# Strassen branch a: storing only the sums of blocks, and splitting the plain blocks during attention

## The chip, the cores and the metric

The kernel runs on one core of one Trainium2 chip. The metric is the device time of one execution in microseconds (us), the median of a few runs.

## The reference

One layer of a hybrid block: an RMS norm, a mixer with two branches, a residual, another RMS norm, a SwiGLU feed-forward layer and a second residual. S = D = 1024, eight heads of 64, all in float32. Cut to the mixer, which is what the change touches:

```python
def mixer(h, w_in, b_f, conv_w, w_branch, w_out):
    proj = jnp.einsum("bsd,dn->bsn", h, w_in)
    q, k, v, f_logit, g_b, g_c, hc, gate_conv, gate_attn = jnp.split(proj, _SPLITS, axis=-1)
    ya = g_b * causal_depthwise_conv(g_c * hc, conv_w)             # 1024 x 512
    yb = forgetting_attention(q, k, v, log_sigmoid(f_logit + b_f)) # 1024 x 512
    ya_d = jnp.einsum("bsc,cd->bsd", ya, w_branch[0])              # branch a
    yb_d = jnp.einsum("bsc,cd->bsd", yb, w_branch[1])              # branch b
    merged = jax.nn.sigmoid(gate_conv) * ya_d + jax.nn.sigmoid(gate_attn) * yb_d
    return jnp.einsum("bsd,de->bse", merged, w_out)
```

## The kernel before

**Numbers.** A float32 product is made of three passes: each operand is kept as a high half and a low half, and `mm3` (line 126) multiplies high by high, high by low and low by high. The halves come from `split` (line 121): ScalarE copies the source to the high half, VectorE subtracts the high half from the source. Most large products, branch a's among them, are also done by Strassen's scheme: seven products of half-size blocks in place of eight, three of them with a plain block on the weight side (A11, A12, A22) and four with sums of blocks (S1 to S4); likewise on the data side, B11, B21, B22 and T1 to T4.

**Stages.** (1) Norm of the input and the projection to v. (2) The other projections: 18 jobs (numbered 0 to 17; 0 to 3 give q and k, 4 to 9 the convolution branch, 10 to 17 the gates), each one call of `strassen` (line 681) of 84 matmuls of 512 columns. The weights of a job are loaded raw from `w_in` in two transfers, `raw_t` (three buffers), while the job before it runs; VectorE forms their sums (tile `sx`) and both engines split them. (3) Attention, in 21 steps t = 0 to 20 with two more for the rest; steps 0 and 1 run inside job 17. In each step from 2 on there are score matmuls (`sp`), transposes (`tps`), the product with v (`po`) and one chunk of branch a's product (`pba`, six matmuls by `a_chunk`, line 1401); six more chunks, `A_TAIL`, come behind the last step. (4) Branch b's product (`pbb`), the merge, w_out, and the feed-forward layer. Stage 4 is not touched.

**Work beside the projections.** TensorE runs job after job in stage 2. Beside it VectorE, ScalarE and the queues prepare operands that later stages need, in small steps. The table at line 1213 says behind which addition of which job a step stands: (j, 0) is behind the first `c12` addition of job j, some 5 us into it, and (j, 1) behind the last `c21` addition at its end. `wa_steps` (762) makes branch a's weight operands from `w_branch`, `ya_steps` (819) its data operands from `ya_dram`, both in two halves k, and `wo_steps` (715) the operands of w_out in four parts. Each loads rows, forms sums, splits, and stores both halves from the GpSimd queue (`wa_dram`, `ya_ops`, `wt_dram`, `w22_dram`). The tiles are few: `r0`, `l0` and `h0` (one buffer each), `yh` and the four rows of `rows4`. So a load of the next part waits until the store of the part before has landed, and since the loads stand on SyncE's queue (SP), what is queued behind them there, the weights of the next job among it, waits with them.

**Order in attention.** From the last job to the end of attention, the instructions of every engine stand in the order in which they are written (`strict[0] = engines`, lines 1285 and 1352); elsewhere only marked VectorE work does, and a scheduler orders the rest. Three tables say what a step does besides: `chunks` (1510, which product), `cuts` (1558, which splits) and `at` (loads and others). Before the change `load_y` and `load_w` fetch all seven operands of either side ready, halves included: 1 MB for one of data, 256 KB for a quarter of one of weights.

Of the kernel before, what the change touches and what calls it, by code (L numbers as in the profile page):

```python
# [46 lines left out]
def block_kernel(  # L47
# [706 lines left out]

    def load_rows(src):
        for n, rows_ in enumerate(src):
            nc.sync.dma_start(rows4[:, n], rows_)

    def wa_rows(k):
        return [w_branch[0, 0][r * P : (r + 1) * P, :] for r in (k, k + 2)]  # L760

    def wa_steps(k):

        def of(op, n):
            return lambda t: wa_dram[op : op + n, :, t, k, :].rearrange("o p c -> p o c")

        tags = deque(("r0", "l0", "h0") * 2)

        def out(op, t):
            n = t.shape[1]  # L770
            h = half_tile(w0_tile(tags.popleft()))[:, :n]
            copy(h, t)
            strict[0] = ("vector",)
            sub(t.bitcast(F32R), t, f32(h))
            strict[0] = ()
            nc.gpsimd.dma_start(of(op, n)(0), f32(h))
            nc.gpsimd.dma_start(of(op, n)(1), t)
# [12 lines left out]
        yield  # L790
        h, l = (half_tile(w0_tile(tags.popleft())) for _ in range(2))
        h4, l4 = (t.rearrange("p o (q c) -> p o q c", q=4) for t in (h, l))
        for n, t in enumerate((a, b)):
            copy(h4[:, n], t[:, 0])
            strict[0] = ("vector",)
            sub(l4[:, n], t[:, 0], f32(h4[:, n]))
            strict[0] = ()
        nc.gpsimd.dma_start(of(4, 2)(0), f32(h))
        nc.gpsimd.dma_start(of(4, 2)(1), f32(l))
        h = half_tile(w0_tile(tags.popleft()))  # L800
        h4 = h.rearrange("p o (q c) -> p o q c", q=4)
        copy(h4[:, 0], b[:, 1])
        strict[0] = ("vector",)
        sub(h4[:, 1], b[:, 1], f32(h4[:, 0]))
        strict[0] = ()
        for t in range(2):
            nc.gpsimd.dma_start(of(6, 1)(t), f32(h[:, t : t + 1]))
        yield
        out(0, s)
        yield  # L810
        if k == 0:
            load_rows(wa_rows(1))
        out(2, u)
        yield

# [3 lines left out]
    def ya_steps(k):  # L819

        def out(op, t):
            n = t.shape[1]
            h = half_tile(z_tile("yh", F32R).rearrange("p (a b) -> p a b", a=2))[:, :n]
            copy(h, t)
            strict[0] = ("vector",)
            sub(t.bitcast(F32R), t, f32(h))
            strict[0] = ()
            for w, x in ((0, f32(h)), (1, t)):
                nc.gpsimd.dma_start(
                    ya_ops[op : op + n, :, w, k, :].rearrange("o p c -> p o c"), x  # L830
                )
# [18 lines left out]
        yield  # L850
        out(2, u)
        yield
# [360 lines left out]
    for first, make in (  # L1213
        (((2, 0), (2, 1), (3, 0), (3, 1)), lambda: wa_steps(0)),
        (((4, 0), (4, 1), (5, 0), (5, 1)), lambda: wa_steps(1)),
        (((10, 1), (11, 0), (11, 1), (12, 0), (12, 1)), lambda: ya_steps(0)),
        (((13, 0), (13, 1), (14, 0), (14, 1), (15, 0)), lambda: ya_steps(1)),
        *(
            (((j, 0), (j, 1), (j + 1, 0), (j + 1, 1)), lambda k=k: wo_steps(k))
            for k, j in enumerate((7, 10, 12, 14))  # L1220
        ),
    ):
        it = make()
        for j, n in first:
            plans[j][n].append(it)
# [3 lines left out]
    for ij, (kind, j, _, _) in enumerate(jobs):  # L1229
# [40 lines left out]
        elif ij < len(jobs) - 1:  # L1270
            if ij == 10:
                load_rows(ya_rows(0))
# [87 lines left out]
    HOME = dict(B11="h0", B21="h1", T2="l0", T3="l1", T4="h0", T1="h1", B22="l1")  # L1360
    wring = deque()

    def load_y(o, queue=nc.sync):
        yops[o] = yq.tile([P, 2, 2, NC], F32R, tag=f"y{HOME[o]}", name=f"y{o}", bufs=1)
        queue.dma_start(f32(yops[o]), ya_ops[SUMS_Y.index(o)])

    def load_w(o, p):
        if not wring:
            wring.extend(("s4", "s4h", "s4h", "s4l", "s4l"))
        tag = wring.popleft()  # L1370
        wops[o, p] = wtile(tag, 1 if tag == "s4" else 2, F32R, (P, 4, P))
        nc.sync.dma_start(
            f32(wops[o, p]),
            wa_dram[SUMS_W.index(o)][:, :, :, p * P : (p + 1) * P].rearrange(
                "p t k c -> p (t k) c"
            ),
        )
# [147 lines left out]
    def next_w():  # L1525
# [3 lines left out]
        (0, 0), (2, 0), (4, 0), (6, 0), (1, 0), (3, 0), (5, 0), (1, 1), (0, 1),  # L1529
        (3, 1), (2, 1), (5, 1), (4, 1), (7, 1), (6, 1), (7, 0),  # L1530
    ])

    def next_sg():
# [25 lines left out]
    for j, parts in (  # L1559
# [18 lines left out]
    for t in (6, 8, 10, 13, 14, 20, 21, 22):  # L1578
        at[t].append(next_sg)
    at[15] += [do(cb_of, 3, 0, True), do(cb_of, 3, 1, True)]  # L1580
    for k, t in enumerate((13, 13, 16, 16)):
        at[t].append(do(load_wb, k))
    rows = {8: (0, None), 13: (1, None), 17: (2, None), 19: (3, 0)}
    for t, (j, part) in rows.items():
        at[t - 1].append(do(inverse, j, part))
        for n in range(2) if part is None else ():
            at[t + 2 + n * (j < 2)].append(do(divide, j, n))
    at[NU].append(do(divide, 3, 0))
# [4 lines left out]
    q_load(1)  # L1593
    load_y("B21")
    for _ in range(3):
        next_w()
# [3 lines left out]
    for t in range(2, NU + 2):  # L1600
# [6 lines left out]
        if t == NU:  # L1607
            early = [a_chunk(*c) for c in chunks.pop(t)]
        if 5 < t <= NU:
# [17 lines left out]
        if t == NU:  # L1627
            for m in early:
                m()
            inverse(3, 1)  # L1630
# [6 lines left out]
        if t > NU:  # L1637
            drain = inverse_rows(3, pss, "T", 2, 1)
            while lows:
                lows.pop(0)()  # L1640
            drain()
        if back:
            dc = turn_bank(back, 1, 0, "ACT" if wide else "DVE")
            dd = turn_bank(back, 1, 1, "DVE" if wide else "ACT")
        for i, e in now[1]:
            row_max(t, i, e)
        if back:
            dc()
# [32 lines left out]
    psm, psm_close = pool("psm2", 6, space=PSUM)  # L1681
    t1_close()

# [4 lines left out]

    TAIL_DONE = len(A_TAIL)
    yb2 = [halves_of(0)]  # L1690
    done = []
    for n, (what, p) in enumerate(A_TAIL):
# [5 lines left out]
        if n == 2:  # L1698
            for m in done[:2]:
                m()  # L1700
            for x in range(2):
                next_sg()
            done[2]()
        if n > 2:
            done[n]()
            if SGS:
                next_sg()
    for n in (1, 0):
# [16 lines left out]
    yb_split(1, range(4))  # L1725
    strict[0] = ()
    yb_close()
    wo_pool, wo_close = pool("wo", side="right")
# [783 lines left out]
```

## Time and profile before

| | |
|---|---|
| median of 3 runs | 1345.71 us (1344.67 to 1351.09) |
| the profiled execution | 1345.25 us, its span 1343.5 us |
| TensorE matmul (PE) | 1308.2 us, 97% of the span, 6671 instructions |
| TensorE weight load (PEld) | 1086.1 us, 81% |
| VectorE (DVE) | 947.5 us, 71% |
| ScalarE (ACT) | 564.5 us, 42% |
| GpSimd (POOL) | 210.4 us, 16% |
| DMA | 245.08 MB in packets, 182 GB/s in the mean |
| mean granted TensorE clock | 0.991 of full speed |

Times count from the start of the span, and 1.75 us of the execution lie outside of it. PE's busy time is not work at its peak: matmuls are pipelined, and back to back one of 512 columns shows 0.39 us but starts every 0.225 us. SP is the queue of SyncE, which here only starts transfers; a row with SPq is its sequencer. What ended an engine's idle time stands in square brackets. All instructions of the kernel bear line 76, the line of a helper, so that they are told apart by the names of their tiles: `b` are the accumulators of a projection job, `hB11`, `hT12` and so on its data operands, `c` its results, `pba` the accumulators of branch a, `um` its results.

### The profile page before, as it was taken

Reading aid. Unit: us, or ns where it says so; the run is one execution under the profiler, and the core shown is the slowest. Engines: PE = TensorE matmul, PEld = TensorE weight load, DVE = VectorE, ACT = ScalarE, POOL = GpSimd, SP = SyncE. Lnnn points to the kernel's source line nnn. Section 1 sums busy time; section 2 is a strip of 40 time slices with the busy share of each in tenths; the row PEclk is TensorE's granted clock in tenths of the full one; section 3 lists DMA queues with packets and bytes.
Section 4 is the critical chain, followed back from the end, with each engine's and each line's share of the span. In section 5 each row is a group of like instructions: output and inputs, shape, how many; then the busy total and the mean of one; then the engine's idle time right before and its main releaser. Section 6 shows DMA issues by size and latency. Waiting matters only on the chain.

```text
span 1343.5 us, 17834 instructions
## 1 busy us (share of the span) xinstructions
PE 1308.2 (97%) x6671; PEld 1086.1 (81%) x6671; DVE 947.5 (71%) x1352; ACT 564.5 (42%) x875; POOL 210.4 (16%) x382
## 2 busy tenths in 40 slices
PE   9999999997889999899999999999999999999998
PEld 8988788886668888778888888888888888888886
DVE  7876878785565677777767788876667656676575
ACT  7533323343334667422577532323222323444452
POOL 3112101122222222000223112210011011000001
PEclk9999999998989999999999999999999999999999
DMA  6355454466864864596467556542333236966541
GB/s 229 102 173 191 170 150 164 156 213 240 268 219 172 283 233 161 158 323 226 107 189 251 188 166 197 184 149 72 110 103 117 96 109 238 359 242 194 165 165 63
DMA packets 184198, 245.08 MB, mean 182 GB/s; under 512 B 12440, under 2 KB 125152, under 8 KB 183216
## 3 DMA queue, kind: packets, MB, share of 16 engines
q1 hardware_dynamic: 157904, 155.03, 36.9%
q0 software_dynamic: 26192, 88.92, 18.0%
q8 instruction: 52, 0.85, 0.3%
q14 instruction: 34, 0.28, 0.1%
q10 hardware_dynamic: 16, 0.00, 0.0%
HBM read 168.09 MB, written 75.83 MB: 182 GB/s over the span
## 4 chain that ended last, share of the span: by engine, by line
PE 72%; issue 18%; POOL 4%; DVE 2%; DMA 2%; ACT 1%; POOLq 0%; DVEq 0%; ACTq 0%; SPq 0%
PE b L76 40%; PE pd L76 16%; PE pbb L76 3%; PE pba L76 3%; PE tps L76 2%; PE po L76 2%; PE sp L76 2%; PE pv L76 1%; PE ma L76 1%; POOL sg_dram L76 1%; PE tp L76 1%; POOL ya_ops L76 1%; DVE lo L76 1%; DMA wa_dram<-r 1%; PE mb L76 1%
## 5 line engine op out<-in xcount | busy, mean ns | idle before, releaser
L76 DVE TENSOR_TENSOR c<-c,b 128x512 f32<-128x512 f32 x215 | 146.8, 683 | 74.2 <-PE b L76 71.4
L76 DVE TENSOR_TENSOR lo<-raw,hi 128x1024 fp32r<-128x1024 f32 (+1 forms) x91 | 109.6, 1205 | 70.5 <-PE b L76 53.1
L76 ACT ACTIVATE hi<-raw 128x1024 fp32r<-128x1024 f32 (+1 forms) x98 | 99.5, 1015 | 93.9 <-PE b L76 54.9
L76 ACT ACTIVATE hi<-sx 128x1024 fp32r<-128x1024 f32 x44 | 46.7, 1061 | 181.5 <-PE b L76 157.6
L76 DVE TENSOR_TENSOR sx<-raw 128x512 f32<-128x512 f32 x78 | 53.7, 689 | 51.8 <-issue 22.5
L76 DVE TENSOR_TENSOR lo<-sx,hi 128x1024 fp32r<-128x1024 f32 x44 | 53.8, 1223 | 38.8 <-PE b L76 31.2
L76 PE MATMUL b<-w12h,lo 128*128 128x512 f32 x208 | 80.9, 389 | 0.0
L76 PE MATMUL b<-w12h,hi 128*128 128x512 f32 x204 | 79.4, 389 | 0.0
L76 PE MATMUL b<-w12l,hi 128*128 128x512 f32 x204 | 79.4, 389 | 0.0
L76 PE MATMUL b<-hh,hi 128*128 128x512 f32 x176 | 69.0, 392 | 0.0
L76 PE MATMUL b<-hh,lo 128*128 128x512 f32 x176 | 68.5, 389 | 0.0
L76 PE MATMUL b<-hl,hi 128*128 128x512 f32 x176 | 68.5, 389 | 0.0
L76 PE MATMUL b<-hT12h,lo 128*128 128x512 f32 x136 | 55.0, 404 | 12.5 <-DVE lo L76 12.5
L76 PE MATMUL b<-w,s4h 128*128 128x512 f32 x208 | 64.1, 389 | 0.0
L76 PE MATMUL pd<-hi,lo 128*128 128x512 f32 x160 | 62.3, 389 | 0.0
L76 PE MATMUL pd<-hi 128*128 128x512 f32 x160 | 61.9, 390 | 0.0
L76 POOL DMA_DIRECT2D a_dramA<-um x33 | 17.9, 542 | 276.0 <-DVE um L76 275.4
L76 PE MATMUL b<-hT34h,hi 128*128 128x512 f32 x136 | 53.9, 396 | 7.3 <-DVE c L76 7.3
L76 PE MATMUL pd<-ghi 128*128 128x512 f32 x148 | 57.6, 390 | 0.0
L76 PE MATMUL pd<-glo,ghi 128*128 128x512 f32 x148 | 57.6, 389 | 0.0
L76 PE MATMUL pd<-ghi,glo 128*128 128x512 f32 x148 | 57.6, 389 | 0.0
L76 PE MATMUL b<-hT12l,hi 128*128 128x512 f32 x136 | 54.1, 398 | 0.0
(479 smaller groups left out, 3606.2 us busy)
## 6 DMA issues: line engine op xcount, KB each, us to landing
raw<-in_w_gate_up_dram SPq DMA_DIRECT2D x52, 512.0 KB, 3.9
raw<-in_w_in_dram SPq DMA_DIRECT2D x35, 512.0 KB, 4.3
a_dramS<-um POOLq DMA_DIRECT2D x44, 256.0 KB, 3.0
a_dramA<-um POOLq DMA_DIRECT2D x33, 256.0 KB, 2.6
sg<-sg_dram SPq DMA_DIRECT2D x32, 256.0 KB, 5.1
graw<-a_dramS SPq DMA_DIRECT2D x14, 512.0 KB, 3.8
sg_dram<-c POOLq DMA_DIRECT2D x24, 256.0 KB, 2.8
raw<-in_w_down_dram SPq DMA_DIRECT2D x11, 512.0 KB, 4.5
```

The source lines that it names most:

```text
L76: ins = getattr(self.engine, name)(*args, **kw)
```

## The change

Only the sums are now formed beside the projections and stored: S1 to S4 and T1 to T4. The plain blocks A11, A12, A22 and B11, B21, B22 are loaded raw in attention, from `w_branch` (tile `wraw`, five buffers of 128x256) and from `ya_dram` (tile `raw`, the ring of three that w_in's weights and the probabilities use), and halved there, a copy on ScalarE and a subtraction on VectorE: A blocks in the step before the one that multiplies with them, B21 in step 2, B22 in step 21, and B11 and the first quarter of A11 ahead of step 2. With fewer steps to place, the table of line 1213 is spaced anew: `wo_steps` starts in jobs 4, 7, 10 and 12 in place of 7, 10, 12 and 14 and takes two to four jobs a part, and `ya_steps` has four steps a half in place of five. The two loads of `ya_dram` rows for `ya_steps` move from SP's queue to GpSimd's. In the last steps of attention, four loads of gates move from the tail to step 17, the drains of the accumulators come ahead of other work of their step, and the divisions by the softmax sums come a step earlier for two of the heads' pairs.

```diff
-    wa_dram = dpool.tile([7, P, 2, 2, NC], F32, name="wa_dram")
-    ya_ops = dpool.tile([7, P, 2, 2, NC], F32, name="ya_ops")
+    wa_dram = dpool.tile([4, P, 2, 2, NC], F32, name="wa_dram")
+    ya_ops = dpool.tile([4, P, 2, 2, NC], F32, name="ya_ops")
...
-    SUMS_W = ("S3", "S2", "S1", "S4", "A11", "A12", "A22")
-    SUMS_Y = ("T1", "T3", "T2", "T4", "B21", "B22", "B11")
+    SUMS_W = ("S3", "S2", "S1", "S4")
+    SUMS_Y = ("T1", "T3", "T2", "T4")
...
+    def spill(dst, op, k, t, h):
+
+        copy(h, t)
+        strict[0] = ("vector",)
+        sub(t.bitcast(F32R), t, f32(h))
+        strict[0] = ()
+        for w, x in ((0, f32(h)), (1, t)):
+            nc.gpsimd.dma_start(dst[op : op + 2, :, w, k, :].rearrange("o p c -> p o c"), x)
...
         if k == 0:
             load_rows(wa_rows(1))
-        out(2, u)
+        spill(wa_dram, 0, k, s, half_tile(w0_tile(("r0", "h0")[k])))
+        yield
+        spill(wa_dram, 2, k, u, half_tile(w0_tile("l0")))
         yield
...
-        out(4, b)
-        out(6, a[:, :1])
+        spill(ya_ops, 0, k, t, staged())
         yield
         if k == 0:
-            load_rows(ya_rows(1))
-        out(0, t)
-        yield
-        out(2, u)
+            load_rows(ya_rows(1), nc.gpsimd)
+        spill(ya_ops, 2, k, u, staged())
...
-            (((j, 0), (j, 1), (j + 1, 0), (j + 1, 1)), lambda k=k: wo_steps(k))
-            for k, j in enumerate((7, 10, 12, 14))
+        (((12, 1), (13, 0), (13, 1), (14, 0)), lambda: wo_steps(3)),
...
+        raws[o] = half_tile(raw_t())
+        m, ns = dict(B11=(0, n1), B21=(2, n1), B22=(2, n2))[o]
+        for k in range(2):
+            queue.dma_start(raws[o][:, k], ya_dram[m + k][:, ns])
+
+    def split_y(o):
+        return halve(yops[o][:, 0], yops[o][:, 1], raws.pop(o))
+
+    def split_w(o, p):
+        w = wops[o, p]
+        return halve(w[:, :2], w[:, 2:], raws.pop((o, p)))
...
+    cuts[2].append(do(split_y, "B21"))
+    cuts[21].append(do(split_y, "B22"))
+    for t, list_ in list(chunks.items()):
+        for c in list_:
+            o = SEQ[c[0]][0]
+            if t > 2 and o not in SUMS_W:
+                cuts[t - 1].append(do(split_w, o, c[1]))
...
+    at[17].append(late_sgs)
...
     load_y("B21")
+    lows = [split_y("B11"), split_w("A11", 0)]
+    for low in lows:
+        low()
...
         if t > NU:
             drain = inverse_rows(3, pss, "T", 2, 1)
-            while lows:
-                lows.pop(0)()
+            for m in muls:
+                m()
+            at[t].pop(0)()
             drain()
+            muls = []
```

How this moves the instructions, at three places. First SP's queue in jobs 10 to 15: `r` and `l` are the rows of w_out, `rows` those of `ya_dram` (`ya_dram_73`, `ya_dram_71`) or of `c_dram`, and `raw<-in_w_in_dram` the weights of the next job. Before:

```order
L76 DMA raw<-in_w_in_dram 128x8x128 x3
L76 DMA r_2781<-in_w_out_dram 128x1024
L76 DMA raw<-in_w_in_dram 128x8x128
L76 DMA rows_970<-ya_dram_73 128x1024
L76 DMA rows_970<-ya_dram_71 128x1024
L76 DMA l_2783<-in_w_out_dram 128x1024
L76 DMA raw<-in_w_in_dram 128x8x128 x3
L76 DMA r_3085<-in_w_out_dram 128x1024
```

and now:

```order
L76 DMA raw<-in_w_in_dram 128x8x128 x4
L76 DMA r_2831<-in_w_out_dram 128x1024
L76 DMA l_2833<-in_w_out_dram 128x1024
L76 DMA raw<-in_w_in_dram 128x8x128 x4
L76 DMA rows_970<-c_dram 128x1024 x2
L76 DMA raw<-in_w_in_dram 128x8x128 x2
```

The two loads of `ya_dram` rows are gone from this queue, and of the loads of w_out's rows only one pair stands between the weights here, where there were two.

Second the same queue at the start of attention, from v's first load on; `yB` and `s` are operands of branch a, `cb` the bias rows, `lo` and the last `raw` k and q of the second pair of heads. Before:

```order
L76 DMA v_3505<-v_dram 128x8x128
L76 DMA yB_3672<-ya_ops 128x2048
L76 DMA s_3674<-wa_dram 128x4x128
L76 DMA cb<-c_dram 128x1024 x2
L76 DMA lo<-qk_dram_67 128x1024
L76 DMA v<-v_dram 128x8x128
L76 DMA raw<-qk_dram_67 128x1024
L76 DMA yB_3686<-ya_ops 128x2048
```

and now:

```order
L76 DMA v_3459<-v_dram 128x8x128
L76 DMA raw<-ya_dram_70 128x512
L76 DMA raw<-ya_dram_71 128x512
L76 DMA wraw<-in_w_branch_dram 128x2x128
L76 DMA cb<-c_dram 128x1024 x2
L76 DMA lo<-qk_dram_67 128x1024
L76 DMA v<-v_dram 128x8x128
L76 DMA raw<-qk_dram_67 128x1024
L76 DMA raw<-ya_dram_72 128x512
L76 DMA raw<-ya_dram_73 128x512
```

B11 and B21 now each take a buffer of the ring `raw`, and stand at the same place in the queue as the ready operands did.

Third VectorE in step 2 of attention, from the last copy of step 1's transposes on (`ISA` rows are the row maxima of the scores, which end in `nm`). Before:

```order
L76 COPY raw<-tps 128x512
L76 ISA rows_970,nm<-sp,rows_970 128x768
L76 ISA nm 128x1
L76 ISA rows_970,nm<-sp,yb 128x128
L76 ISA nm 128x1
L76 COPY ptT<-tps 128x384
```

and now:

```order
L76 COPY raw<-tps 128x512
L76 TENSOR_TENSOR yB_3626<-raw,yB_3626 128x1024
L76 TENSOR_TENSOR s_3630<-wraw,s_3630 128x256
L76 ISA rows_970,nm<-sp,rows_970 128x768
L76 ISA nm 128x1
L76 ISA rows_970,nm<-sp,yb 128x128
L76 ISA nm 128x1
```

The subtractions for B11 and A11 stand ahead of the row maxima of step 2 (on ScalarE their copies stand ahead of that step's first copy of transposes).

More of the change, by code (lines that the diff above doesn't have):

```diff
@@ L753, in quarter, with load_rows @@
         return rows4[:, n].rearrange("p (a b) -> p a b", a=2)
-    def load_rows(src):
+    def load_rows(src, queue=nc.sync):
         for n, rows_ in enumerate(src):
-            nc.sync.dma_start(rows4[:, n], rows_)
+            queue.dma_start(rows4[:, n], rows_)
     def wa_rows(k):
         return [w_branch[0, 0][r * P : (r + 1) * P, :] for r in (k, k + 2)]
-    def wa_steps(k):
[L764 to L777, printed above, removed]
+    def spill(dst, op, k, t, h):
[5 more added lines that the diff above has]
+            nc.gpsimd.dma_start(dst[op : op + 2, :, w, k, :].rearrange("o p c -> p o c"), x)
+    def wa_steps(k):
         a, b = (
@@ L790, in wa_steps @@
         yield
[L791 to L807, printed above, removed]
-        yield
-        out(0, s)
-        yield
         if k == 0:
             load_rows(wa_rows(1))
-        out(2, u)
+        spill(wa_dram, 0, k, s, half_tile(w0_tile(("r0", "h0")[k])))
+        yield
+        spill(wa_dram, 2, k, u, half_tile(w0_tile("l0")))
         yield
@@ L819, in ya_steps, with staged @@
     def ya_steps(k):
[L821 to L831, printed above, removed]
+        def staged():
+            return z_tile("yh", F32R).rearrange("p (a b) -> p a b", a=2)
         a, b, t, u = (quarter(n) for n in range(4))
@@ L1213, in block_kernel @@
     for first, make in (
[L1214 to L1218, printed above, removed]
-            (((j, 0), (j, 1), (j + 1, 0), (j + 1, 1)), lambda k=k: wo_steps(k))
-            for k, j in enumerate((7, 10, 12, 14))
-        ),
+        (((2, 0), (2, 1), (3, 0)), lambda: wa_steps(0)),
+        (((3, 1), (4, 0), (4, 1)), lambda: wa_steps(1)),
+        (((4, 1), (5, 0), (5, 1), (7, 0)), lambda: wo_steps(0)),
+        (((7, 1), (8, 0), (8, 1), (10, 0)), lambda: wo_steps(1)),
+        (((10, 1), (11, 0), (11, 1), (12, 0)), lambda: wo_steps(2)),
+        (((12, 1), (13, 0), (13, 1), (14, 0)), lambda: wo_steps(3)),
+        (((10, 1), (11, 1), (12, 0), (12, 1)), lambda: ya_steps(0)),
+        (((13, 1), (14, 0), (14, 1), (15, 0)), lambda: ya_steps(1)),
     ):
@@ L1271, in block_kernel @@
             if ij == 10:
-                load_rows(ya_rows(0))
+                load_rows(ya_rows(0), nc.gpsimd)
             if ij == 16:
@@ L1360, in block_kernel @@
     HOME = dict(B11="h0", B21="h1", T2="l0", T3="l1", T4="h0", T1="h1", B22="l1")
-    wring = deque()
+    wring, raws = deque(), {}
     def load_y(o, queue=nc.sync):
-        yops[o] = yq.tile([P, 2, 2, NC], F32R, tag=f"y{HOME[o]}", name=f"y{o}", bufs=1)
-        queue.dma_start(f32(yops[o]), ya_ops[SUMS_Y.index(o)])
+        yops[o] = t = yq.tile(
+            [P, 2, 2, NC], F32R, tag=f"y{HOME[o]}", name=f"y{o}", bufs=1
+        )
+        if o in SUMS_Y:
+            queue.dma_start(f32(t), ya_ops[SUMS_Y.index(o)])
+            return
+        raws[o] = half_tile(raw_t())
[7 more added lines that the diff above has]
+        return halve(w[:, :2], w[:, 2:], raws.pop((o, p)))
     def load_w(o, p):
@@ L1371, in load_w @@
         wops[o, p] = wtile(tag, 1 if tag == "s4" else 2, F32R, (P, 4, P))
+        if o in SUMS_W:
+            nc.sync.dma_start(
+                f32(wops[o, p]),
+                wa_dram[SUMS_W.index(o)][:, :, :, p * P : (p + 1) * P].rearrange(
+                    "p t k c -> p (t k) c"
+                ),
+            )
+            return
+        m, c = (0 if o == "A11" else 2), (2 * p + (o == "A22")) * P
+        raws[o, p] = t1.tile([P, 2, P], F32, tag="wraw", name="wraw", bufs=5)
         nc.sync.dma_start(
[L1373 to L1376, printed above, removed]
+            raws[o, p],
+            w_branch[0, 0][m * P : (m + 2) * P, c : c + P].rearrange("(k p) c -> p k c", p=P),
         )
@@ L1529, in block_kernel, with late_sgs @@
         (0, 0), (2, 0), (4, 0), (6, 0), (1, 0), (3, 0), (5, 0), (1, 1), (0, 1),
-        (3, 1), (2, 1), (5, 1), (4, 1), (7, 1), (6, 1), (7, 0),
+        (3, 1), (5, 1), (2, 1),
     ])
+    def late_sgs():
+        for ds_ in ((7, 7), (4, 6)):
+            t = t1.tile([P, S], F32, tag="cb", name="sg", bufs=2)
+            for d, n in zip(ds_, range(2)):
+                sgs[d, n if d == 7 else 1] = t[:, (n1, n2)[n]]
+                nc.sync.dma_start(
+                    sgs[d, n if d == 7 else 1], sg_dram[d][0][:, (n1, n2)[n if d == 7 else 1]]
+                )
     def next_sg():
@@ L1607, in block_kernel @@
         if t == NU:
-            early = [a_chunk(*c) for c in chunks.pop(t)]
+            for m in [a_chunk(*c) for c in chunks.pop(t)]:
+                m()
         if 5 < t <= NU:
@@ L1627, in block_kernel @@
         if t == NU:
-            for m in early:
-                m()
             inverse(3, 1)
@@ L1646, in block_kernel @@
             row_max(t, i, e)
+        if t == NU - 1:
+            for m in muls:
+                m()
+            muls = []
         if back:
@@ L1681, in block_kernel @@
     psm, psm_close = pool("psm2", 6, space=PSUM)
-    t1_close()
     def yb_split(n, ks):
@@ L1698, in block_kernel @@
         if n == 2:
-            for m in done[:2]:
+            for m in done:
                 m()
-            for x in range(2):
-                next_sg()
-            done[2]()
         if n > 2:
             done[n]()
-            if SGS:
-                next_sg()
+    assert not SGS and not w_order
     for n in (1, 0):
@@ L1726, in block_kernel @@
     strict[0] = ()
+    t1_close()
     yb_close()
```

5 lines of the change are left out of this document (2 added, 3 removed).

## The prediction

> **What bounds the kernel now.** I read the page first, for the engine that is busy throughout:
>
> ```profile
> PE 1308.2 (97%) x6671; PEld 1086.1 (81%) x6671; DVE 947.5 (71%) x1352; ACT 564.5 (42%) x875; POOL 210.4 (16%) x382
> ```
>
> TensorE is the bound, and the change leaves its matmuls as they are. So time can only come from stretches in which it waits, and can only go into waits that are new. The windows show where it does less than the usual 222 instructions in 50 us:
>
> ```profile
> 300.00:350.00 50.00, 40.15 (x169) 32.13 (x167) 29.79 (x41) 17.35 (x24) 12.63 (x22) 0.93 0.71 248
> 350.00:400.00 50.00, 41.91 (x168) 33.73 (x167) 30.73 (x41) 16.70 (x22) 12.19 (x21) 0.90 0.72 243
> 600.00:650.00 50.00, 50.00 (x222) 41.40 (x221) 36.67 (x53) 13.61 (x22) 5.64 (x7) 1.00 0.58 190
> ```
>
> PE's timeline names each wait of over 1 us from job 2 to the end of attention, and the first matmul of a job gives the jobs' lengths:
>
> ```profile
> 117.67 0.39 PE L76 MATMUL b<-hB11h,hi 128*128 128x512 f32 x1
> 135.97 0.50 PE L76 MATMUL b<-hT34h,hi 128*128 128x512 f32 x1 [1.82 <-DVE c L76]
> 139.19 0.48 PE L76 MATMUL b<-hB11h,hi 128*128 128x512 f32 x1
> ...
> 291.77 0.39 PE L76 MATMUL b<-hB11h,hi 128*128 128x512 f32 x1
> 310.81 0.39 PE L76 MATMUL b<-hB11h,hi 128*128 128x512 f32 x1
> 323.14 0.80 PE L76 MATMUL b<-hT12h,lo 128*128 128x512 f32 x1 [6.27 <-DVE lo L76]
> 323.73 0.63 PE L76 MATMUL b<-hT12h,hi 128*128 128x512 f32 x1
> 324.15 0.63 PE L76 MATMUL b<-hT12l,hi 128*128 128x512 f32 x1
> 338.13 0.50 PE L76 MATMUL b<-hT34h,hi 128*128 128x512 f32 x1 [2.82 <-DVE c L76]
> 372.63 0.79 PE L76 MATMUL b<-hT12h,lo 128*128 128x512 f32 x1 [5.47 <-DVE lo L76]
> 388.23 0.80 PE L76 MATMUL b<-hT34h,hi 128*128 128x512 f32 x1 [2.62 <-DVE c L76]
> 392.40 0.39 PE L76 MATMUL b<-hB11h,hi 128*128 128x512 f32 x1
> ...
> 555.84 1.67 PE L76 MATMUL pba<-yT,s4l 128*128 128x512 f32 x6 [1.16 <-DVE um L76]
> ...
> 562.19 0.74 PE L76 MATMUL tps<-ident,rows 128*128 128x128 f32 x5 [1.14 <-DVE um L76]
> 567.75 2.25 PE L76 MATMUL pba<-yT,s4h 128*128 128x512 f32 x6 [2.05 <-DVE um L76]
> 580.09 1.63 PE L76 MATMUL pba<-yB,s4h 128*128 128x512 f32 x6 [2.50 <-DMA s4h<-wa_dram]
> ```
>
> Job 12 is undisturbed: 310.81 - 291.77 = 19.04 us. Jobs 13 to 15 take 392.40 - 310.81 = 81.59 us, 24.5 above three times 19.04, and job 3 takes 21.52, 2.5 above. Of the 24.5 the four waits are 17.2; most of the rest is TensorE at a lower clock when it restarts (0.42 us from 323.73 to the next start, 0.225 when warm).
>
> Why jobs 13 and 15 wait: their weights came late. SP's queue, that transfer's landing beside the usual one, and the VectorE row that waited for it:
>
> ```profile
> 303.49 1.66 SPq L76 DMA_DIRECT2D rows<-ya_dram  x2
> 305.30 0.37 SPq L76 DMA_DIRECT2D l<-in_w_out_dram  x1
> 305.77 31.01 SPq L76 DMA_DIRECT2D raw<-in_w_in_dram  x3
> ```
> ```profile
> raw<-in_w_in_dram SPq DMA_DIRECT2D x1, 512.0 KB, 12.8
> ```
> ```profile
> raw<-in_w_in_dram SPq DMA_DIRECT2D x35, 512.0 KB, 4.3
> ```
> ```profile
> 318.61 0.69 DVE L76 TENSOR_TENSOR sx<-raw 128x512 f32<-128x512 f32 x1 [11.14 <-issue]
> ```
> ```profile
> 300.00:310.00 10.00, 10.00 (x46) 8.29 (x45) 6.55 (x8) 3.11 (x5) 4.09 (x7) 1.00 0.99 353
> ```
>
> The transfer left 14 us into job 12, behind the rows of ya and of w_out, and took 12.8 us on DMA engines that were 99% busy. Without the 6.27 us of idle time `sx<-raw` would have had to start at 318.61 - 6.27 = 312.3, that is 20.5 us after job 12 began: this is the weights' deadline, and with the usual 4.3 us they must leave by 16.2 us. The later wait of both jobs has another cause, an ACT copy that waits for a store out of the single buffer `h`; job 3's is of that kind too, in the chain of waits:
>
> ```profile
> 332.89 1.06 ACT L76 ACTIVATE h<-r 128x1024 fp32r<-128x1024 f32 x1 [7.36 <-DMA w_dram<-h]
> ```
> ```profile
> 123.39 8.19 DMA wa_dram<-r
> ```
>
> **The change part by part.** *Projections.* Three of seven operand pairs go on each side, 3 MB of stores each, and the row loads leave SP. The step that stores out of `h` and the split that needs it again stood about a quarter of a job apart; now they stand some 13 us apart, which covers the 7.36 us: the second waits end. Job 3's plain split, which reused `r`, is gone. If all goes, 24.5 + 2.5 = 27.0 us are won. What is late next: in SP's queue `r` and `l` now stand together ahead of the second weights of a job. Both wait for stores of the w_out part before, which by the order leave GpSimd some 8 us into the job; if such a store takes as long as a load (4.3 us) or half again, the weights leave at about 14.5 and land at 19, or at 23 with half of the 8.5 us that the late ones took on top. Deadline 20.5. I charge 2 us for job 13, 1.5 for job 15, 0.5 for clock: 4 (bounds 0 and 12). Term: -23.
>
> *Start of attention.* The ready operands of P1 were long there; now B11 comes through the ring `raw`, and its load must wait until the probabilities of step 1 in the oldest buffer have been transposed. That point is visible, since the q load was the first to wait for it:
>
> ```profile
> 438.38 0.32 SPq L76 DMA_DIRECT2D raw<-qk_dram  x1
> ```
> ```profile
> 440.14 1.69 PE L76 MATMUL pba<-yB,s 128*128 128x512 f32 x6
> ...
> 442.52 0.39 PE L76 MATMUL sp<-hi 64*128 64x256 f32 x2
> ...
> 444.87 1.75 PE L76 MATMUL po<-ptT,v 128*64 128x128 f32 x28
> ```
> ```profile
> 437.57 0.96 DVE L76 CUSTOM_DVE_ANT_0 rows<-sp,rows 128x768 f32<-128x768 f32 x1 [1.02 <-PE sp L76]
> ...
> 440.22 0.08 DVE L76 DVE_READ_ACCUMULATOR2_ANT nm<- 128x1 f32 x1
> 442.63 0.56 DVE L76 COPY ptT<-tps 128x384 f32<-128x384 f32 x1 [2.33 <-PE tps L76]
> ```
> ```profile
> L76 DVE TENSOR_TENSOR lo<-raw,hi 128x1024 fp32r<-128x1024 f32 (+1 forms) x91 | 109.6, 1205 | 70.5 <-PE b L76 53.1
> L76 ACT ACTIVATE hi<-raw 128x1024 fp32r<-128x1024 f32 (+1 forms) x98 | 99.5, 1015 | 93.9 <-PE b L76 54.9
> ```
>
> B11's halves leave at 438.4 and 438.8 and land after some 4.3 us at 443.1. Then ScalarE's copy 1.0 (444.1), VectorE's subtraction 1.2 (445.3) and the 128x256 one of A11, no row of which exists: between a quarter of 1.2 and 1.2, I take 0.4 (445.7). The row maxima of step 2 stand behind this on VectorE (437.57 to 440.30, 2.7 us) and end at 448.4 instead; the scores of step 3 need the last of them, so 448.4 instead of 442.52: +5.9. Behind that ScalarE has the exponentials (1.7), the halves of k (1.1), B21 (1.0), a block of A (0.4) and then the copy of transposes (0.6) that PE's next row needs: from the maximum at 446.5 that is 451.3, and `po` follows at 451.7, not 444.87: +6.8. TensorE idles 4 us or so from 440.2 on, long enough for a slow restart: seven matmuls 0.2 us late each, as from 323.73, +1.4. Term: +8. Bounds: +5 (3.0 us to land, 0.3 for the small row, no slow restart) and +11 (the loads behind each other, 1 us twice, and the small rows at their full price).
>
> The Trainium skill (TensorE: Matmul & The Clock Gate, What's actually happening) says that after about 3.4 us without work the array's clock falls to half, and that about 3.4 us of work bring it back. The rows agree in part: behind 6.27 and 5.47 us the first matmul shows 0.80 and 0.79, behind 2.82 only 0.50, but behind 2.62 it is 0.80 as well, so that the gap alone does not decide. The rule gives the same 1.4 us for a gap of 4 us and nothing for one under 3.4.
>
> *Inside attention.* Twelve small splits and the two further large ones (1.0 on ScalarE, 1.2 on VectorE) stand in steps whose VectorE waits 2 us for transposes (440.30 to 442.63 in step 2); they hide there, 0. Without that cover it is 12 x 0.4 = 5 us. The loads fall from 6 MB to 3 MB: 0.
>
> *End of attention.* Drains come ahead of other work: the wait of 1.16 stays (its VectorE work is the same), that of 1.14 goes, of 2.05 some 0.6 is left, but the first chunk with B22 waits for its split (+0.8). The 2.50 us wait is for this load:
>
> ```profile
> 571.90 8.05 DMA s4h<-wa_dram
> ```
>
> It stood behind gate loads that are now in step 17, leaves about 4 us earlier and shall leave 0.75; clock 0.6. Term: -1.14 - 1.45 + 0.8 - 1.75 - 0.6 = -4.1 (bounds -6 and -1).
>
> *Sum.* -23 + 8 - 4.1 = -19.1. The profiled execution took 1345.25 us, 0.46 below the median of the runs shown, so 1326 for either.
>
> **The rivals.** *A: contention stays.* The weights' 12.8 us came from full DMA engines rather than from their place in SP's queue; the rows still move, now on another queue at the same time, and only 3 of 7 stores are gone. If the waits of 6.27 and 5.47 us stay with 2 us of restart each, 16 of the 27 stay: -11 + 8 - 4 = -7, 1338. For it: 0.99 of DMA, and the rows leave in the same part of job 12. Against it: 1.5 MB less is 4 us less at 353 GB/s, and these were the only late weights. The Trainium skill (DMA: Bandwidth & Descriptors, Issuing engines are not separate DMA queues) has it that transfers of all issuing engines share the same 16 DMA engines, so that another queue saves the issue time alone; by that rule only the missing bytes help.
>
> *B: no price at the start of attention.* B11 lands as soon as 441, or steps catch up: -27 - 5 + 1, 1314. Against it: PE has no slack there (97%), and SP's order is fixed.
>
> *C: slower.* `r` and `l`, now in jobs 7, 10 and 12 just ahead of the weights, hold SP's queue past 16.2 us into the job, since GpSimd's stores are late behind its own row loads. That such a wait exists is shown in 300 to 400 us:
>
> ```profile
> SPq L76 <- DMA wt_dram<-l: 5.7, 1, 5.7
> ```
>
> If the weights of jobs 8, 11 and 13 leave 9 us too late, each of these jobs stalls by 9 and 2 of restart: -27 - 4 + 8 + 33 = +10, 1355. It decides once the three stalls exceed 23 us in all, 7.7 each. Against it: these stores leave in the first half of a job.
>
> That the change doesn't do what it says I leave out: the stores and loads are gone from the queues.
>
> **How the numbers follow.** Forecast 0.58 (1326, its own range 1318 to 1334: ends of the second and third terms and half the residue), A 0.20, B 0.14, C 0.08. The range 1312 to 1340 takes in B and A; outside is C and little more. 0.5% (6.7 us) is about what a measurement of this kernel tells from no change: under 1339.0 is faster. Forecast, B and 0.12 of A: 0.84. Within: the rest of A and a little of C, 0.10. Slower: 0.06.
>
> **What would show it.** Right: jobs 3 and 13 to 15 at 19 to 22 us in PE's timeline; no ACT row waiting for `w_dram`; PE idle about 4 us before the first `pba` and the first `sp` of step 3 about 8 us after `pba` would have begun; `s4h` waited for under 1 us. Wrong: weights still landing over 20.5 us after the start of job 12 or 14, a wait for `sx<-raw` in jobs 8 or 11, or the first `pba` starting without a gap.

## The result, and the profile after

The changed kernel takes 1334.03 us in the median (1333.80 to 1337.93, five runs) against 1345.71 (1341.92 to 1351.09, five runs): a ratio of 0.992, 95% interval 0.9891 to 0.9949. It is faster, by 11.7 us where 19 were forecast. The profiled execution took 1335.76 us, with a span of 1334.0 against 1343.5, so that the traces show 9.5 us of the 11.7. Two executions in a slower state, of 2662.87 us in experiment 3 and of 2193.06 us in experiment 8, are left out of the times below.

The busy times on the page have hardly moved; only TensorE's share is higher, because its waits are fewer:

```profile
PE 1307.5 (98%) x6671; PEld 1086.3 (81%) x6671; DVE 948.4 (71%) x1357; ACT 565.1 (42%) x880; POOL 203.0 (15%) x371
```

PE's timeline after, with the starts of jobs 12, 13 and 16, and the waits of over 0.6 us from job 13 to the end of attention. The row at 530.00 is a place late in attention that both kernels have, a `pba` that waits 0.67 us: behind it only the end of attention and stage 4 are left. (Columns: start, busy time, instruction, count, and in brackets the wait ahead of it and what ended it.) After:

```profile
291.00 0.39 PE L76 MATMUL b<-hB11h,hi 128*128 128x512 f32 x1
310.05 0.39 PE L76 MATMUL b<-hB11h,hi 128*128 128x512 f32 x1
319.83 0.80 PE L76 MATMUL b<-hT12h,lo 128*128 128x512 f32 x1 [3.73 <-DVE lo L76]
372.97 0.39 PE L76 MATMUL b<-hB11h,hi 128*128 128x512 f32 x1
425.38 2.93 PE L76 MATMUL pba<-yB,s 128*128 128x512 f32 x6 [4.58 <-ACT s L76]
436.25 0.90 PE L76 MATMUL tps<-ident,rows 128*128 128x128 f32 x3 [4.86 <-ACT ptT L76]
437.08 3.26 PE L76 MATMUL po<-ptT,v 128*64 128x128 f32 x28
530.00 1.68 PE L76 MATMUL pba<-yT,s 128*128 128x512 f32 x6 [0.67 <-DVE rT L76]
551.18 1.21 PE L76 MATMUL pba<-yT,s4l 128*128 128x512 f32 x4 [0.87 <-DVE s4l L76]
557.52 0.50 PE L76 MATMUL pba<-yB,s4h 128*128 128x512 f32 x1 [0.87 <-ACT yB L76]
558.78 1.43 PE L76 MATMUL pba<-yB,s4h 128*128 128x512 f32 x5 [0.76 <-DVE yB L76]
```

and that `pba` before:

```profile
535.31 1.66 PE L76 MATMUL pba<-yT,s 128*128 128x512 f32 x6 [0.67 <-DVE rT L76]
```

With the job starts of both timelines the 9.5 us of the spans come apart into three stretches, which are also the three terms of the forecast's sum:

| stretch | before | after | change | forecast |
|---|---|---|---|---|
| job 2 to job 16 (start 98.63 to 392.40; 98.72 to 372.97) | 293.77 | 274.25 | -19.5 | -23 |
| job 16 to the `pba` with the 0.67 us wait | 142.91 | 157.03 | +14.1 | +8 |
| from there to the end of the span | 808.2 | 804.0 | -4.2 | -4.1 |

In the projections job 3 fell from 21.5 to 19.4 us, job 13 from 30.2 to 24.5, job 14 from 20.1 to 19.05 and job 15 from 31.3 to 19.4; job 5 is new with 20.4. The start of attention has two waits, and slow matmuls behind each: six `pba` show 2.93 us where they showed 1.69.

### The profile page after: what moved, and what is told of

The parts are those of the page before. It is cut to its first block, busy times and chain, and to the rows that moved or that the text cites. A ratio compares the mean times of both kernels' runs of the same rounds, so it can differ in the third digit from the quotient of the medians.

```text
span 1334.0 us, 17816 instructions
## 1 busy us (share of the span) xinstructions
PE 1307.5 (98%) x6671; PEld 1086.3 (81%) x6671; DVE 948.4 (71%) x1357; ACT 565.1 (42%) x880; POOL 203.0 (15%) x371
## 4 chain that ended last, share of the span: by engine, by line
PE 92%; DVE 4%; DMA 2%; issue 1%; SPq 1%; ACT 0%; DVEq 0%; POOLq 0%; POOL 0%; ACTq 0%
PE b L76 57%; PE pd L76 16%; PE pv L76 3%; PE pbb L76 3%; PE pba L76 3%; PE tps L76 2%; PE po L76 2%; PE sp L76 2%; PE tp L76 1%; DMA raw<-in_w_in_dram 1%; PE ma L76 1%; DVE lo L76 1%; PE mb L76 1%; DMA raw<-ya_dram 1%; SPq L76 1%
## 5 line engine op out<-in xcount | busy, mean ns | idle before, releaser
L76 PE MATMUL b<-hT12h,hi 128*128 128x512 f32 x136 | 53.4, 393 | 0.0
```

The costliest lines, as they stand in the source:

```text
L76: ins = getattr(self.engine, name)(*args, **kw)
```

## The experiments

All comparisons are with the kernel before, run beside each on the same chip; the ratios have 95% intervals. Job lengths are differences of job starts in PE's timeline.

**1. B11 and B21 in buffers of their own.** My theory on the second stretch: the loads of B11 and B21 wait for the ring `raw`, SP's queue stands behind them, and then everything leaves at once. The rival: it is the splits themselves, ahead of the row maxima. What SP's queue waits for in 415 to 440 us, in the changed kernel, and its timeline there:

```profile
SPq L76 <- PE tps L76: 19.5, 1, 19.5
```
```profile
418.99 0.81 SPq L76 DMA_DIRECT2D raw<-ya_dram  x2
...
422.42 3.86 SPq L76 DMA_DIRECT2D raw<-qk_dram  x1
426.45 0.79 SPq L76 DMA_DIRECT2D raw<-ya_dram  x2
```

The queue stood for 19.5 us, and B21 (426.45) left only behind 2.6 MB of other loads, 7.5 us behind B11. ScalarE's copies of B11 and of B21 are the rows that waited for these loads; behind the second stands the copy of transposes (`ptT`) that ends TensorE's second wait:

```profile
423.40 1.06 ACT L76 ACTIVATE yB<-raw 128x1024 fp32r<-128x1024 f32 x1 [5.71 <-DMA raw<-ya_dram]
...
434.35 1.06 ACT L76 ACTIVATE yB<-raw 128x1024 fp32r<-128x1024 f32 x1 [3.89 <-DMA raw<-ya_dram]
```

The tiles `yl0` and `yl1` stand empty until step 6:

```diff
-        raws[o] = half_tile(raw_t())
+        if o == "B22":
+            raws[o] = half_tile(raw_t())
+        else:
+            raws[o] = f32(yq.tile([P, 2, 2, NC], F32R, tag=dict(B11="yl0", B21="yl1")[o], name="yraw", bufs=1)[:, 0])
```

> The changed kernel, with the raw blocks B11 and B21 loaded into two operand tiles that stand empty until step 6 of attention, not into the ring of three raw buffers. Theory 1 (the ring holds SP's queue until step 1's probabilities are transposed, and 5 MB of loads then leave in one burst): SP is free at about 399 us, B11 lands before 410, both waits of TensorE (4.58 us before the first pba, 4.86 us in the middle of the next transposes) and the slow restarts behind them go, some 14 us: about 1320 us. Theory 2 (the splits that stand ahead of the row maxima of step 2 on VectorE and ScalarE are the cost, whenever their data come): the row maxima still wait for 1.6 us of subtractions and the block copies, the waits shrink by a third at most, about 1329 us or more.

Measured: 1323.88 us, ratio 0.9845 (0.9826 to 0.9865). SP's timeline, then PE's:

```profile
403.30 1.00 SPq L76 DMA_DIRECT2D yraw<-ya_dram  x2
404.48 0.38 SPq L76 DMA_DIRECT2D wraw<-in_w_branch_dram  x1
404.96 1.00 SPq L76 DMA_DIRECT2D cb<-c_dram  x2
```
```profile
376.84 0.39 PE L76 MATMUL b<-hB11h,hi 128*128 128x512 f32 x1
...
430.55 0.33 PE L76 MATMUL tps<-ident,rows 128*128 128x128 f32 x1 [1.47 <-ACT ptT L76]
...
521.49 0.50 PE L76 MATMUL pba<-yT,s 128*128 128x512 f32 x1 [0.67 <-DVE rT L76]
```

The second stretch is 144.65 us: of 14.1 us 1.7 are left, 1.47 of them one wait. What is left for the splits themselves, all of them, is 0.3 us. Theory 1 holds; that the time is some 4 us over its 1320 is in part job 5, which lasts 23.0 us here.

**2. The order of the burst alone.** Is B21 late because of what stands ahead of it? Here the raw blocks stay in the ring, and branch a's loads go ahead of the others:

```diff
     load_y("B11")
     next_w()
+    load_y("B21")
+    for _ in range(3):
+        next_w()
     load_kv(1)
     q_load(1)
-    load_y("B21")
...
-    for _ in range(3):
-        next_w()
```

> The changed kernel, with the raw blocks still in the ring of three, but all of branch a's loads at the start of attention (B11, A11, B21 and three quarters of A blocks) ahead of the bias rows, k, v and q in SP's queue. Theory 1 (two causes of about equal size: the ring holds the queue, then the burst of loads ahead of B21 makes it late): the first wait of 4.6 us stays, B21 lands some 8 us earlier, the second wait of 4.9 us goes with its restart, 1326 to 1329 us. Theory 2 (the ring alone, or the splits): both waits stay, or the second moves to k's late halves, 1332 to 1336 us.

Measured: 1335.69 us, ratio 0.9914 (0.9892 to 0.9935), the changed kernel's time. Here theory 1 fell, with the variant that theory 2 names: the second wait is 4.23 us, and ScalarE's row says that it is now k that lands late:

```profile
436.27 1.15 ACT L76 ACTIVATE hi<-lo 128x512 fp32r<-128x512 f32 x2 [5.06 <-DMA lo<-qk_dram]
```

Some 5 MB leave in this burst, k and B21 are needed soon after one another, and whichever stands last is late. So the second wait goes with the burst as a whole, not with B21's place in it. The changed kernel's windows show how full the DMA engines were (the columns: busy time and instructions of PE, PEld, DVE, ACT and POOL, then TensorE's granted clock, the DMA engines' busy share, and GB/s):

```profile
420.00:426.00 6.00, 1.42 (x18) 1.08 (x14) 1.51 (x3) 1.96 (x3) 0.00 (x0) 0.95 0.82 271
426.00:432.00 6.00, 5.39 (x35) 4.20 (x34) 4.47 (x12) 2.56 (x6) 0.90 (x2) 0.77 1.05 376
432.00:438.00 6.00, 1.75 (x13) 1.42 (x15) 2.56 (x5) 3.65 (x9) 0.18 (x1) 0.80 0.84 272
438.00:444.00 6.00, 6.00 (x39) 4.94 (x39) 1.93 (x8) 3.21 (x9) 0.73 (x2) 0.63 0.08 23
```

**3. The row loads' queue, alone on the kernel before, and taken back in the changed one.** Two edits that test the same thing, the place of ya's rows in SP's queue (two calls of two transfers each):

```diff
-            load_rows(ya_rows(1))
+            load_rows(ya_rows(1), nc.gpsimd)
...
-                load_rows(ya_rows(0))
+                load_rows(ya_rows(0), nc.gpsimd)
```

On the kernel before:

> The kernel before, with only the loads of ya's rows moved from SP's queue to GpSimd's. Theory 1 (bytes and tile reuse made the late weights): jobs 13 and 15 still last 28 us or more, the waits for w_dram stores stay, 1340 to 1346 us. Theory 2 (SP's queue made them): the weights of both jobs leave 2 to 6 us earlier and land in time, the waits of 6.27 and 5.47 us go with their restarts, about 1330 to 1334 us.

and the reverse edit on the changed kernel:

> The changed kernel, with the loads of ya's rows moved back from GpSimd's queue to SP's. Theory 1 (job 13's remaining wait of 3.73 us comes from a busy set of DMA engines and from the load of w_out's rows that holds SP, not from the rows' queue): jobs 13 to 15 change by under 3 us in all, 1332 to 1337 us. Theory 2 (the place of these loads in SP's queue was the main cause of the 24.5 us that the kernel before lost): weights behind them leave late again, jobs 13 and 15 lose 8 us or more each, 1345 us or more.

Measured: on the kernel before 1345.92 us, ratio 1.0009 (0.9995 to 1.0023), jobs 13 and 15 at 29.2 and 30.7; in the changed kernel 1333.17, ratio 0.9917 (0.9900 to 0.9933), jobs 13 and 15 at 23.8 and 19.2. Theory 1 in both: this part of the change does nothing measurable. The Trainium skill (DMA: Bandwidth & Descriptors, Issuing engines are not separate DMA queues) says that transfers of all issuing engines run on the same DMA engines and that another queue saves only the issue; these two runs agree.

**4. The bytes put back.** The changed kernel, storing in addition as many bytes of ya's operands as before, to scratch that nobody reads:

```diff
+            if dst is ya_ops:
+                m = 2 - op // 2
+                more = dst[4 + op : 4 + op + m, :, w, k, :].rearrange("o p c -> p o c")
+                nc.gpsimd.dma_start(more, x[:, :m])
```

> The changed kernel, which also stores three operand pairs' worth of bytes more per half of ya's operands (1.5 MB each, to a part of the scratch memory that nobody reads), on GpSimd's queue at the places where it stores now; ya's stores are then as many bytes as in the kernel before, and nothing else is put back. Theory 1 (bytes): the weights of jobs 13 and 15, on DMA engines that are full, land some 4 us later, job 13 lasts 28 us and job 15 over 22: 1340 to 1345 us. Theory 2 (order, waits and tiles, not bytes): jobs as in the changed kernel within 2 us, 1334 to 1336 us.

Measured: 1338.91 us, ratio 0.9960 (0.9945 to 0.9974), about 5 us over the changed kernel. All five executions (1338.07 to 1341.10) are longer than the three of experiment 3 with the same stores as the changed kernel (1332.16 to 1335.77). Job 13 lasts 26.8 us and job 15 20.3: both theories' bounds are missed, and the truth lies between. Job 13's weights in the chain of waits of this run, and in that of the changed kernel:

```profile
304.39 13.04 DMA raw<-in_w_in_dram
```
```profile
306.78 9.60 DMA raw<-in_w_in_dram
```

One pair of traces says little, since experiment 8 shows the same order vary by as much. Over all of them the two groups don't meet: from its issue to VectorE's row that reads it, this load takes 12.5 to 13.5 us in the five traces with all of ya's stores (the kernel before, this one, the first of experiment 3, experiments 5 and 6) and 6.1 to 11.3 us in the nine others (though four of the five differ from these in more than the stores). Jobs 10 to 15 take 123.3 us against 120.0 in the changed kernel. So ya's bytes are worth 3 us by these jobs and 5 by the medians, a sixth to a quarter of what the projections won.

**5. w_out's spacing alone.** The kernel before, all seven operands stored, with w_out's steps spaced in jobs 10 to 14 as in the changed kernel:

```diff
-        *(
-            (((j, 0), (j, 1), (j + 1, 0), (j + 1, 1)), lambda k=k: wo_steps(k))
-            for k, j in enumerate((7, 10, 12, 14))
-        ),
+        (((7, 0), (7, 1), (8, 0), (8, 1)), lambda: wo_steps(0)),
+        (((9, 0), (9, 1), (10, 0), (10, 1)), lambda: wo_steps(1)),
+        (((10, 1), (11, 0), (11, 1), (12, 0)), lambda: wo_steps(2)),
+        (((12, 1), (13, 0), (13, 1), (14, 0)), lambda: wo_steps(3)),
```

> The kernel before, all seven operands stored as before, with only w_out's steps spaced as widely in jobs 10 to 14 as in the changed kernel (its second part moved to jobs 9 and 10 for room). Theory 1 (the spacing of these steps is the larger part of the 19 us gained in the projections, the bytes the smaller, 4 to 5 us): the waits behind the single buffer h go, job 15 falls to 23 us or less, job 13 to 28 or less, 1330 to 1337 us. Theory 2 (bytes and the omitted steps made the gain): jobs 13 and 15 within 3 us of before, 1341 to 1347 us.

Measured: 1339.06 us, ratio 0.9944 (0.9928 to 0.9959). Jobs 10 to 15 take 130.2 us against 138.7 before and 120.0 in the changed kernel; job 15 falls to 24.0, job 13 only to 28.5, and jobs 10 to 12 together lose 1.6. The time lies between the ranges of both theories. The spacing alone is worth 8.5 us there, the largest part tried by itself, if less than theory 1 had it.

**6. The edits at the end of attention alone,** on the kernel before: the four gate loads, the drains ahead of the step's other work, and the divisions. (By the expression below only one division moves, the first of the third pair of heads, from step 19 to 18; those of the first two pairs keep their steps.)

```diff
+    at[17].append(late_sgs)
...
-            at[t + 2 + n * (j < 2)].append(do(divide, j, n))
+            at[t + 1 + n + (j < 2)].append(do(divide, j, n))
...
-            while lows:
-                lows.pop(0)()
+            for m in muls:
+                m()
+            at[t].pop(0)()
             drain()
```

> The kernel before, with only the edits at the end of attention (four gate loads in step 17, drains ahead of other work, divisions a step earlier). Theory 1 (these edits alone are worth what the two traces show between the last step's products and branch b, 4 us): 1341 to 1342 us, the waits of 1.14, 2.05 and 2.50 us gone. Theory 2 (the gain there comes from the lighter loads of branch a's blocks): the wait for the last weights stays, under 2 us gained, 1343 to 1346 us.

Measured: 1339.52 us, ratio 0.9948 (0.9933 to 0.9963). The span is 1338.3 us and the `pba` with the 0.67 us wait stands at 537.10, so that the last stretch takes 801.2 us against 808.2: 7.0 us, more than theory 1 said. The changed kernel has won only 4.2 there. It gives 2.8 back, and its three waits at 551.18, 557.52 and 558.78, where it splits the last A22 block and B22, sum to 2.5. (In the other traces with this end of attention the last stretch takes 802.8 to 804.9 us.)

**7. Three attempts at the rest.** First all that seemed to help: experiment 1, B21 and the A blocks ahead of q, steps of w_out's last three parts earlier by half a job or a job (two of its first part's later by as much), B22's split a step earlier.

```diff
+        (((4, 1), (5, 1), (6, 1), (7, 0)), lambda: wo_steps(0)),
+        (((7, 1), (8, 0), (8, 1), (9, 1)), lambda: wo_steps(1)),
+        (((9, 1), (10, 0), (10, 1), (11, 0)), lambda: wo_steps(2)),
+        (((12, 0), (13, 0), (13, 1), (14, 0)), lambda: wo_steps(3)),
```

> The changed kernel with what the runs so far point to: B11 and B21 in the two empty operand tiles, B21 and the A blocks ahead of q in SP's queue, w_out's steps half a job to one job earlier (so that its last loads leave in job 11 and the load at job 4 has a job to land), and the split of B22 a step earlier. Theory 1: the waits of jobs 5 and 13 go (2 and 5 us), the remaining 1.5 us at the start of attention and 1.6 us at its end too, about 1314 us, 2% under the kernel before. Theory 2 (job 13's weights are late because of the bytes of its own stretch, whenever w_out's loads leave): job 13 keeps 3 us or more, 1318 to 1322 us.

Measured: 1322.92 us, ratio 0.9826 (0.9811 to 0.9841). Jobs 5 and 13 are clean (19.1 and 19.0), but jobs 10 and 11 together lost 6.9 and job 8 1.8, since the next part's sums now stood ahead of their load on VectorE:

```profile
268.80 0.43 DVE L76 CAST h<-l 128x512 fp32r<-128x512 f32 x1 [5.22 <-DMA l<-in_w_out_dram]
```

The weights of job 13, with no loads of w_out's rows left in job 12, took 6.1 us. Neither theory had the loss: too little distance between a part's last store and the next one's first use.

Then experiment 1 with B21 and the A blocks ahead of q and w_out's last two loads on GpSimd's queue:

```diff
-            nc.sync.dma_start(flat(t), wout_d[row * P : (row + 1) * P, :])
+            (nc.gpsimd if k == 3 else nc.sync).dma_start(
+                flat(t), wout_d[row * P : (row + 1) * P, :]
+            )
```

> The changed kernel with B11 and B21 in the two empty operand tiles, B21 and the A blocks ahead of q in SP's queue, and the two loads of w_out's last part on GpSimd's queue, not ahead of job 13's weights on SP's. Theory 1 (job 13's remaining wait has two halves, the load of w_out's rows that holds SP until 15.8 us into job 12, and 9.6 us of landing on full DMA engines): the weights leave about 12 us into job 12 and land near 21, job 13 falls from 24 to 21 us or less, and the 1.5 us left at the start of attention go: 1317 to 1320 us, less what job 5 adds (1 to 4 us, it varies). Theory 2 (full DMA engines alone): the weights leave earlier but land no earlier than 24 us, job 13 stays at 24: 1321 to 1324 us.

and the same with w_out's first two parts later by half a job:

```diff
-        (((4, 1), (5, 0), (5, 1), (7, 0)), lambda: wo_steps(0)),
-        (((7, 1), (8, 0), (8, 1), (10, 0)), lambda: wo_steps(1)),
+        (((4, 1), (5, 1), (7, 0), (7, 1)), lambda: wo_steps(0)),
+        (((7, 1), (8, 1), (9, 1), (10, 0)), lambda: wo_steps(1)),
```

> As the run with w_out's last loads on GpSimd's queue, and w_out's first part begins its sums half a job later (behind the last addition of job 5, not the first), its second part likewise, so that their rows have landed. Theory 1: VectorE no longer stands in front of a load in job 5, its 1 to 4 us go, nothing else changes: 2 us under that run, near 1316 us. Theory 2 (VectorE's work in jobs 5 to 9 is too dense, any place of these sums makes a wait): jobs 7 to 10 lose what job 5 gains, within 1 us of that run.

Measured: 1323.44 us, ratio 0.9831 (0.9808 to 0.9854), and 1315.81 us, ratio 0.9775 (0.9749 to 0.9801). In both the start of attention has no wait over 0.3 us left. In the first, job 13's weights left 12.4 us into job 12, 3.4 us earlier than in the changed kernel, but took 11.2 us, so that they landed 23.5 us into it (25.4 there), job 13 at 23.8: theory 2. In the second job 5 is clean as meant, and job 13 too, which nothing in the edit explains: its weights left at the same 12.4 us and landed after 7.6. So only part of the difference between the two times is the edit's.

**8. B22 earlier, and the best kernel again.** On the kernel of 1315.81 us, B22's load in step 18 and its split in step 19:

```diff
-    cuts[21].append(do(split_y, "B22"))
+    cuts[19].append(do(split_y, "B22"))
...
-    at[19].append(do(load_y, "B22", nc.gpsimd))
+    at[18].append(do(load_y, "B22", nc.gpsimd))
```

> As the run with w_out's loads on GpSimd's queue and its sums half a job later (median 1315.8 us), with B22's load in step 18, not 19, and its split in step 19, not 21. Theory 1 (of the 7.0 us that the edits at the end of attention win alone, the changed kernel gives back 2.8 because the splits of B22 and of the last A22 block stand ahead of their products there): the waits of 0.87 and 0.76 us for B22 go, that of 0.87 for A22 stays, about 1.7 us under that run, 1314 us. Theory 2 (the 2.8 us are the last steps' density on ScalarE and VectorE, wherever the split stands): the waits go and others of the same sum come, within 0.7 us of that run.

Measured: 1320.66 us, ratio 0.9809 (0.9789 to 0.9828). The last stretch gained 0.7 us of the 1.7 (two waits of 0.95 and 0.59 us took the place of the two for B22): by the waits theory 2, though 0.7 us is no more than this stretch varies between traces. The time is longer because job 13 lasts 23.1 us and job 3 21.4, though the order of instructions there is the same. So the kernel of 1315.81 us once more:

> The kernel of the 1315.8 us once more, unchanged. Its projections have the same order of instructions as those of the run with B22's split in step 19, in which the weights of job 13 left at the same 12.4 us into job 12 and landed 10.5 us later instead of 7.6, and job 13 lasted 23.1 us instead of 19.04. Theory 1 (what the full DMA engines make of the same order varies from one loading of a program to the next): the time is anywhere from 1315 to 1322 us, with job 13 or job 3 longer than 20 us when it is over 1318. Theory 2 (it goes with the program): 1314.5 to 1318.5 us again, all jobs at 19.0 to 19.4 us.

Measured, on another chip: 1318.76 us, ratio 0.9801 (0.9777 to 0.9824), with executions from 1315.86 to 1322.26; in the profiled one, the longest, job 13 is at 24.0 and job 3 at 20.9. The times are as theory 1 has them; that they go with the loading is not shown, since these five alone differ by 6.4 us. Job 13's weights in the chain of waits of this run, and where it did not wait, the row of VectorE that ended its wait for them (11.14 us to land here, 7.6 there):

```profile
303.60 11.14 DMA raw<-in_w_in_dram
```
```profile
309.86 0.69 DVE L76 TENSOR_TENSOR sx<-raw 128x512 f32<-128x512 f32 x1 [4.36 <-DMA raw<-in_w_in_dram]
```

With both runs this kernel is about 2% under the kernel before and 1% under the changed one; the one with B22 earlier is not told apart from it.

## Why the prediction was right, and where its sizes were off

The forecast had the sign, the three terms and most of their mechanisms; 1334.03 lies at the upper end of its own 1318 to 1334, between its 1326 and rival A's 1338. The first two terms missed by 3.5 and 6.1 us, both the same way. One of the signs of being wrong came: job 13's weights landed 25.4 us into job 12, not by 20.5, and job 13 lasts 24.5 us. The second term, at +14.1, lies outside the bounds of +5 and +11 that it was given.

*Projections, -23 forecast, -19.5 measured.* Of 27.0 us in all 4 were to stay, as late weights behind `r` and `l`; 7.5 stayed. Job 13's weights left 15.8 us into job 12 where I had 14.5, and took 9.6 us where I had up to 8.5 in all: 5.5 us in place of 2 for job 13. Job 15, charged 1.5, kept 0.3. Job 5's 1.3 us I had not seen: VectorE stands in front of a load of w_out's rows, and job 5 is clean once the sums come half a job later (experiment 7).

```profile
165.50 0.43 DVE L76 CAST h<-l 128x512 fp32r<-128x512 f32 x1 [1.61 <-DMA l<-in_w_out_dram]
```

Where the gain came from I had only in part: the forecast puts stores, the row loads' queue and the reuse of `h` side by side. The runs give the queue nothing, ya's bytes 3 to 5 us, w_out's spacing alone 8.5; the other 6 to 8 (branch a's weight stores and the steps left out among them) were not tried by themselves. Rival A was right that the landing stays long while the DMA engines are full (a share of 0.98 from 300 to 310 us), and wrong on how much of the stall stays.

*Start of attention, +8 forecast, +14.1 measured.* This is the step that failed: the sum has no term for B21's landing; "land after some 4.3 us" is used for B11 and, unsaid, for B21. For B11 it nearly held (4.4 us from its first issue to ScalarE's copy, and a first wait of 4.58 where I had about 4). But I let B21's landing be no bound at all and took ScalarE's row of work for it, with `po` 6.8 us late. B21 took 7.9 us from its first issue to ScalarE's copy, which stood 3.89 us for it, and `po` was 11.6 us late (437.08, where the distance from job 16 before gives 425.44). The queue released at the end of step 1 had 5 MB to send, which at the 376 GB/s of the busiest window take 13 us; B21's copy began 15.4 us after the release. And I counted one slow restart, 1.4 us; there were two, and 14.1 less the waits (9.4) less the 0.3 of the splits leaves 4.4 for them. The rows add up to the same: against their times in the kernel before and in experiment 1, those behind the first wait lost 1.6 us, those behind the second 2.8. The clock's granted share was 0.77, 0.80 and 0.63 of full speed in the three windows of 6 us from 426 on. The Trainium skill (TensorE: Matmul & The Clock Gate, What's actually happening) puts the fall after about 3.4 us of idleness; both waits are longer than that, and the 1.47 us wait of experiment 1 left no slow row behind (0.33 us, and the six `pba` behind it 1.66), which agrees. An estimate from that section's figures, 3.4 us of work at half speed, prices a restart at 1.7 us, where the prediction wrote that the rule gives the same 1.4. The second restart cost more than either, and the length of the wait does not decide alone: behind 2.62 us (before, 388.23) and behind 2.40 us (experiment 8, B22 earlier) the first matmul shows 0.80 and slow rows follow, behind the 2.82 us of the kernel before none do. There the traces differ from the rule, and they decide.

*Inside attention, 0.* Right, to within the 0.3 us that experiment 1 leaves for all splits.

*End of attention, -4.1 forecast, -4.2 measured.* Right as a sum, and that by luck, since two misses of some 2 us cancel: the drains, the division and the gate loads are worth 7.0 us, not 4.9, and the splits of A22 and B22 cost 2.8, not 0.8. That other waits came when B22's split moved two steps earlier fits last steps that are too dense for it; it is not shown.

What stays open: why the same kernel lands job 13's weights after 7.6 us in one trace and after 11.1 in another. It is worth 5 us, as much as several of the edits. The runs show that it is not the edit, no more; whether it goes with the loading, the chip or the single execution they don't tell.

## What to carry to other kernels

A load that replaces a ready operand needs a buffer that is free early: look at who reads the buffer last, and at everything behind that load in its queue, for the queue pays the wait once and the burst behind it a second time. Price a landing in such a place by the bytes that leave together over the bandwidth of a full window, not by the median landing. Move work off a hot stretch by its spacing first: here it was worth 8.5 us, the bytes 3 to 5, and the issuing queue nothing. Compare an edit of a few us over several executions, since one kernel's differ by 6.4.

## What the runs showed of the hardware

With the DMA engines full (a busy share of 0.97 to 1.02 from 300 to 310 us in the changed kernel, in experiment 4, in the last two kernels of experiment 7 and in experiment 8), job 13's 512 KB load took 7.6 to 13.0 us where the median of its kind was 4.3 before, and its time varied by 3.5 us between two traces of the same kernel. Moving the four loads of ya's rows, 2 MB, from SP's queue to GpSimd's changed nothing (1.0009, interval 0.9995 to 1.0023). In the burst at the start of attention, with the DMA engines 82% to 105% busy, one issue on SP's queue took 3.86 us, where most take 0.3 to 0.5. Two waits of under 5 us cost TensorE another 4.4 us at a lower clock. The first matmul behind a wait does not tell whether the clock falls: behind the 3.07 us of experiment 8's last trace it shows 0.50, as behind the 2.82 us of the kernel before, but rows of 0.61 to 0.63 begin 1.0 us later.
